# A depthwise convolution tile moved from VectorE to TensorE between the blocks of an mLSTM

## The chip, the cores and the metric

The kernel runs on one core of a Trainium2 chip. The metric is the device time of one execution in microseconds (us). An execution is built from five engines that run their own instruction streams and wait for each other by semaphores: TensorE (PE), VectorE (DVE), ScalarE (ACT), GpSimd (POOL) and SyncE (SP, which here issues most loads).

## The reference

The program is a two-layer backbone on 512 latent and 256 context tokens of width 1024. Only the mixer of layer 0 is touched. It runs a convolution module and a bidirectional mLSTM on the same normed input, and projects both together:

```python
def _dwconv(x, w, b):
    k, ch = w.shape
    pad = (k - 1) // 2
    y = lax.conv_general_dilated(x, w[:, None, :].astype(x.dtype), (1,), [(pad, k - 1 - pad)],
                                 dimension_numbers=('NWC', 'WIO', 'NWC'), feature_group_count=ch)
    return y + b
...
    def merge(p, h_seq):
        a, g, _, _, _, o, _, _ = p
        u = _dwconv(a * jax.nn.sigmoid(g), conv_w, conv_b)
        u = jax.nn.silu(_layer_norm(u, ln_g, ln_b))
        hm = _rms(h_seq).transpose(0, 2, 1, 3)
        hm = hm.reshape(*hm.shape[:2], -1).astype(o.dtype) * head_gain * jax.nn.sigmoid(o)
        return jnp.concatenate([u, hm], axis=-1) @ w_out
```

The convolution is 31 taps wide on 512 channels, so four tiles of 128 channels. `h_seq` is the sum of a forward and a backward mLSTM scan over the tokens, four heads of 128 values each. The layer norm is over all 512 channels: it needs all four tiles.

## The kernel before

All 768 tokens stand along the free dimension, channels along the 128 partitions. A projection (`proj`, `mm`, L110) multiplies in three products, high by high, low by high and high by low, where `weights` (L158 to L168) loads 512 KB of weights (`wr`), rounds them to `wh` on ScalarE and subtracts to `wl` on the engine `lo_eng`, three buffers of each in a ring. `lo_eng` is GpSimd from the start of the mixer to its end. One 128-channel projection of all tokens is 48 matmuls of 384 columns.

`mixer0` (L533 to L737) is written in this order, and the engines keep roughly to it: the projection pair of convolution tile 0 (`glu(0)`: `pa` times the sigmoid of `pg`, whose halves are scaled into `up`), the gates (`pgt`), `glu(1)`, the queries and keys, `glu(2)` and `glu(3)`, then the values (`vproj`, `pv`), among whose four groups of 36 matmuls five units of the modulation vectors are computed (`ada_pe`: 1 MB loads `wa`, matmuls `pada`, a copy `arow` on ScalarE, transposes `pac`, and the bias add into `mods`, on VectorE); one unit is left behind the values. Each `glu` hands its tile to `conv_taps` (L589 to L595): ScalarE writes the first tap into `acc`, VectorE adds the 30 others, one instruction of 783 columns each, called out a few at a time (`TAP`) between the projections. `F` in the order string flushes what is left of them.

Then PSUM is laid out anew (`MLSTM`: two buffers of two banks for `S`, two for `M`), and the string `PAT0` sets the order of three generators: `o`, four output-gate projections (`po`); `m`, the mLSTM, which is five backward state updates (`pu`) and then six steps, each of scores (`pst`), the masked exponentials (`ex`, a DMA, GpSimd and four ScalarE instructions for each of two directions), the readout (`pn`), a forward update, and behind every second step a `finish` (a reciprocal root in small VectorE instructions, eight ScalarE scales of `hu`, transposes `pht` and the gate product into `so`); and `l`, the layer norm (L889 to L938): three adds of tiles, the mean product `pm`, four subtracts, four squares `lsq` with their sum rows `pr`, a root, a broadcast product `pb`, and for each tile a scale, a tanh, an affine step, a product and the split into `uh` and `ul`. Two of the four tiles run on GpSimd. The output projection (`pab`, eight tiles of 48 matmuls) takes the four `uh` as its first half and the mLSTM's `hm` as its second; its first `MH` tiles do their `uh` half ahead of the end of the mLSTM. Everything behind it (the feed-forward part, layer 1) is not touched.

The order string and the way in which a letter becomes work:

```python
PAT0 = 'F' + 'ooommmmmollll' + 'ml' * 22
...
            gens = {"o": [gate_o()], "m": [cell], "l": [ln]}
```

Of the kernel before, what the change touches and what calls it, by code (L numbers as in the profile page):

```python
# [16 lines left out]
P = 128  # L17
# [14 lines left out]
CW = 31  # L32
# [15 lines left out]
MH = 2  # L48
# [3 lines left out]
PAT0 = 'F' + 'ooommmmmollll' + 'ml' * 22  # L52
# [19 lines left out]
MLSTM = {"S": (2, 2), "M": (2, 2)}  # L72
# [8 lines left out]
class Net:  # L81
# [206 lines left out]
    def ada_cols(self, rows, layer, mod, k1):  # L288

        p2 = self.psum1("pac")  # L290
        for k in range(4):
            self.mm(p2[:, 2 * k:2 * k + 2], rows[:, k * P:(k + 1) * P], self.selq, True, True)
        self.ada_bias(p2, layer, mod, k1, 4)

    def ada_first(self, h, pool):

        w = self.d["ada_w"][0]
        for mod in (1, 0):
# [7 lines left out]
            self.ada_cols(self.ada_rows(ps), 0, mod, 4 * h)  # L306
# [61 lines left out]
    def ada_bias(self, p2, layer, mod, k1, n):  # L368
        o = self.mods[layer][:, mod, k1:k1 + n, :]
        k0 = mod * KD + k1  # L370
        b = self.adab[layer][:, k0:k0 + n].unsqueeze(2).to_broadcast([P, n, 2])
        pv = p2[:, :2 * n].rearrange("p (k v) -> p k v", v=2)
        if mod in (1, 4):
            tmp = self.small.tile([P, KD, 2], F32, tag="amod", name=self.name("amod"))[:, :n]
            self.tt(tmp, pv, b, ALU.add)
            self.nc.vector.tensor_scalar(o, tmp, 1.0, None, op0=ALU.add)
        else:
            self.tt(o, pv, b, ALU.add)
# [36 lines left out]
    def setup_c(self, st, sl):  # L415
# [16 lines left out]
        nc.vector.tensor_copy(ab, pa[:, 16:64])  # L432
        self.adab.append(ab)
# [37 lines left out]
    def params(self, st, n):  # L471
# [11 lines left out]
        nc.vector.tensor_scalar(v2[:, 88:89], v2[:, 88:89], float(QK) ** -0.5, None, op0=ALU.mult)  # L483
        self.adab.append(ab)
# [48 lines left out]
    def mixer0(self, pes):  # L533
# [3 lines left out]
        with ExitStack() as es:  # L537
# [60 lines left out]

            def glu(ct):
# [42 lines left out]
            for ct in (2, 3):  # L642
                for _ in glu(ct):
                    self.step(TAP)
                self.step(TAP)
            v1 = self.vproj(win, hs, mods)
# [5 lines left out]
            pes.close()  # L652
            pes = ExitStack()
            self.psum_pool(pes, MLSTM)
# [13 lines left out]
            gens = {"o": [gate_o()], "m": [cell], "l": [ln]}  # L668

            def run(kind):  # L670
                while gens[kind]:
# [3 lines left out]
                    if kind == "c":  # L675
                        return
# [8 lines left out]
            while gens["l"]:  # L685
                run("l")
# [29 lines left out]
            for m in range(KD - KDL):  # L716
                k0 = 4 if m < MH else 0
                w = self.weights(wout, k0, KD - k0, m * P, P)
                ps = pss[m] if m < MH else self.pt("MS"[m // 2 % 2], "pab")[:, 512 - T // 2:512 + T // 2]
# [169 lines left out]
    def layer_norm(self, accs, uh, slot, pslot):  # L889
# [3 lines left out]
        def eng(ct):  # L893
            return nc.gpsimd if ct < 2 else nc.vector
# [45 lines left out]
    def mlstm(self, G, q, k, v1, so, mp):  # L940
# [13 lines left out]
        def update(i, t, old, new):  # L954

            ps = self.pt("M", "pu")
# [629 lines left out]
```

## Time and profile before

| | us |
|---|---|
| median of three runs | 1783.05 |
| lowest, highest | 1782.91, 1785.39 |
| the profiled execution, its own time | 1782.59 |
| span of its profile | 1780.8 |
| PE, DVE, ACT, POOL busy in the span | 1679.1, 1130.3, 679.2, 246.0 |

PE is busy for 94% of the span; the shares of the engines say little of the mixer, which is some 400 us of it. A row of the timeline is start, duration, engine, line, operation, what is written and what is read (names without numbers), its size, how many were joined (x), and in brackets the idle time before it and whose end released it. PE's ends are modelled, so neighbouring matmuls overlap in it: the start-to-start time is the cost.

### The profile page before, as it was taken

What the parts mean: (1) busy time and instruction counts of PE and PEld (TensorE: products, weight loads), DVE (VectorE), ACT (ScalarE), POOL (GpSimd) and SP (SyncE); (2) the same over time, 40 slices, a digit from 0 to 9 for tenths busy, and PEclk for the clock granted to TensorE, in tenths of its full rate; (3) what the DMA queues carried; (4) which work ended last, traced back from release to release, by engine and by line L of the source; (5) the groups of instructions that cost most, each with busy time, mean ns of one, the idle gap of its engine ahead of it and who ended that gap; (6) DMA issues with size and microseconds to landing.
All of it is one profiled execution on the core that took longest, in us unless ns stands there. A gap on an engine that the chain in (4) does not pass through costs nothing.

```text
span 1780.8 us, 24171 instructions
## 1 busy us (share of the span) xinstructions
PE 1679.1 (94%) x9436; PEld 1519.1 (85%) x9436; DVE 1130.3 (63%) x1743; ACT 679.2 (38%) x1364; POOL 246.0 (14%) x331
## 2 busy tenths in 40 slices
PE   6998698769999999999999998999999799999999
PEld 3998476659899999999999878999988788888887
DVE  3799964745876555474334487777788854444544
ACT  4421042542331221212222346777876442332232
POOL 2342132425100000000000111223140200000000
PEclk8999799779999999999999999999999899999999
DMA  9621442233253345262221332001110133333332
GB/s 311 216 61 42 135 143 83 61 118 100 74 159 106 108 142 166 84 200 67 64 60 49 97 96 61 32 13 36 44 35 25 36 95 97 101 98 95 95 95 83
DMA packets 194747, 168.43 MB, mean 95 GB/s; under 512 B 8552, under 2 KB 168214, under 8 KB 194632
## 3 DMA queue, kind: packets, MB, share of 16 engines
q1 hardware_dynamic: 191936, 163.30, 29.8%
q0 software_dynamic: 1280, 3.35, 0.8%
q8 instruction: 75, 1.23, 0.3%
q10 hardware_dynamic: 1416, 0.21, 0.1%
q14 instruction: 40, 0.33, 0.1%
HBM read 161.55 MB, written 5.29 MB: 94 GB/s over the span
## 4 chain that ended last, share of the span: by engine, by line
PE 81%; DVE 10%; DMA 3%; ACT 3%; issue 1%; POOL 1%; SPq 0%; ACTq 0%; DVEq 0%; POOLq 0%
PE pfo L110 17%; PE pfg L110 16%; PE pfv L110 16%; DVE acc L593 6%; PE psc L110 4%; PE pab L110 3%; PE ppv L110 2%; PE pt L1409 2%; PE po L110 2%; PE pf L110 2%; PE pmo L110 2%; PE puq L110 2%; PE pukv L110 2%; PE pv L110 1%; PE pn L110 1%
## 5 line engine op out<-in xcount | busy, mean ns | idle before, releaser
L113 ACT ACTIVATE wh<-wr 128x1024 fp32r<-128x1024 f32 (+3 forms) x205 | 204.4, 999 | 625.0 <-PE pfo L110 215.5
L167 DVE TENSOR_TENSOR wl<-wr,wh 128x1024 fp32r<-128x1024 f32 (+3 forms) x171 | 195.8, 1147 | 194.4 <-ACT wh L113 190.5
L110 PE MATMUL pfo<-hh,wh 128*128 128x384 f32 (+2 forms) x528 | 166.8, 355 | 0.0
L110 PE MATMUL pfo<-hl,wh 128*128 128x384 f32 (+2 forms) x528 | 166.6, 355 | 0.0
L110 PE MATMUL pfo<-hh,wl 128*128 128x384 f32 (+2 forms) x528 | 166.2, 354 | 0.0
L110 PE MATMUL pfg<-fh,wh 128*128 128x384 f32 (+1 forms) x504 | 152.0, 355 | 0.0
L110 PE MATMUL pfg<-fl,wh 128*128 128x384 f32 (+1 forms) x504 | 151.6, 354 | 0.0
L110 PE MATMUL pfg<-fh,wl 128*128 128x384 f32 (+1 forms) x504 | 151.2, 354 | 0.0
L110 PE MATMUL pfv<-fh,wl 128*128 128x384 f32 (+1 forms) x504 | 150.8, 353 | 0.0
L110 PE MATMUL pfv<-fl,wh 128*128 128x384 f32 (+1 forms) x504 | 150.8, 353 | 0.0
L110 PE MATMUL pfv<-fh,wh 128*128 128x384 f32 (+1 forms) x504 | 150.7, 353 | 0.0
L119 DVE SCALAR_TENSOR_TENSOR xr<-pfo,mods,xr 128x512 f32<-128x512 f32 (+1 forms) x128 | 83.7, 665 | 104.4 <-PE pfo L110 103.8
L593 DVE SCALAR_TENSOR_TENSOR acc<-up,par,acc 128x783 f32<-128x783 f32 x120 | 146.9, 1249 | 4.4 <-ACT acc L113 2.3
L167 POOL TENSOR_TENSOR wl<-wr,wh 128x1024 fp32r<-128x1024 f32 (+1 forms) x34 | 85.3, 2512 | 296.9 <-ACT wh L113 280.2
L253 POOL TENSOR_TENSOR ss<-ss,sq 128x256 f32<-128x256 f32 (+1 forms) x31 | 32.1, 1044 | 573.5 <-ACT sq L113 572.6
L119 DVE SCALAR_TENSOR_TENSOR ga<-gr,cc,ga 128x1024 f32<-128x1024 f32 (+1 forms) x84 | 96.0, 1161 | 22.6 <-DMA gr<-in_ada_w_dram 22.3
L110 PEld LDWEIGHTS pfo<-hl,wh 128*128 128x128 f32 x528 | 98.1, 189 | 8.9 <-issue 0.2
L110 PEld LDWEIGHTS pfo<-hh,wh 128*128 128x128 f32 x528 | 97.9, 189 | 9.0 <-ACT hh L113 0.4
L110 PEld LDWEIGHTS pfo<-hh,wl 128*128 128x128 f32 x528 | 97.9, 189 | 8.7
L116 DVE TENSOR_TENSOR ft<-ft,pfv 128x768 f32<-128x768 f32 (+1 forms) x42 | 34.4, 820 | 109.9 <-PE pfv L110 109.9
L110 PEld LDWEIGHTS pfg<-fh,wh 128*128 128x128 f32 x504 | 92.8, 189 | 6.5
L110 PEld LDWEIGHTS pfg<-fl,wh 128*128 128x128 f32 x504 | 92.8, 189 | 6.4
(418 smaller groups left out, 3711.0 us busy)
## 6 DMA issues: line engine op xcount, KB each, us to landing
wr<-in_ffn_w_in_dram SPq DMA_DIRECT2D x88, 512.0 KB, 4.0
gr<-in_ada_w_dram SPq DMA_DIRECT2D x48, 512.0 KB, 4.5
wa<-in_ada_w_dram SPq DMA_DIRECT2D x20, 1024.0 KB, 8.1
wr<-in_ffn_w_out_dram SPq DMA_DIRECT2D x32, 512.0 KB, 3.5
wr<-in_ab_w_in_dram SPq DMA_DIRECT2D x20, 512.0 KB, 5.2
wr<-in_ffn_w_out_dram SPq DMA_DIRECT2D x24, 384.0 KB, 3.3
gr<-in_ada_w_dram SPq DMA_DIRECT2D x16, 256.0 KB, 2.7
wr<-in_mla_w_out_dram SPq DMA_DIRECT2D x8, 512.0 KB, 3.4
```

The source lines that it names most:

```text
L110: self.nc.tensor.matmul(out, lhsT=lhsT, rhs=rhs, start=start, stop=stop)
L113: self.nc.scalar.activation(out, in_, func, **kw)
L116: self.nc.vector.tensor_tensor(out, a, b, op=op)
L119: self.nc.vector.scalar_tensor_tensor(out, a, s, b, op0=op0, op1=op1, **kw)
L167: self.lo_eng.tensor_tensor(lo[:, :n], raw[:, :n], hi[:, :n].bitcast(F32), op=ALU.subtract)
L253: eng.tensor_tensor(self.ss[:, s:e], self.ss[:, s:e], sq[:, s:e], op=ALU.add)
L593: nc.vector.scalar_tensor_tensor(acc[:, :CONVO], up[:, k:k + CONVO], self.convw[:, 4 * k + ct:4 * k + ct + 1], acc[:, :CONVO], op0=ALU.mul ...
L1409: nc.tensor.transpose(pt[:, o:o + P], pe[:, (j + jj) * P:(j + jj + 1) * P], self.ident)
```

## The change

Convolution tile 3 is no longer projected ahead of the values but behind them, as a fourth generator `c`. Its taps are done on TensorE: each tap is a 128 by 128 diagonal matrix (the identity scaled by that tap's column, made by ScalarE), multiplied with the shifted input, in the same three products of high and low parts, 31 taps by 3 products by 512 and 256 columns into one PSUM tile `pcv`, six taps (`DG`) to a letter `c`. ScalarE then adds the convolution's bias on the way out of PSUM. The other parts: the whole mixer keeps one PSUM ring of four two-bank buffers; the low halves of weights go to VectorE from the values on; the layer norm runs wholly on VectorE; the bias of the `ada_pe` units is added by ScalarE, in four instructions of two columns (the `1 +` is folded into the table once); the output projection starts one tile ahead instead of two.

```diff
-MH = 2
+MH = 1
-PAT0 = 'F' + 'ooommmmmollll' + 'ml' * 22
+PAT0 = 'F' + 'cc' + 'mmmmm' + 'mc' * 3 + 'mo' * 4 + 'mc' * 4 + 'mll' * 11
+DG = 6
-MLSTM = {"S": (2, 2), "M": (2, 2)}
...
-        self.ada_bias(p2, layer, mod, k1, 4)
+        self.ada_bias(p2, layer, mod, k1, 4, on_act)
...
+        if on_act:
+            for k in range(n):
+                self.act(o[:, k], pv[:, k], AF.Identity, bias=b[:, k:k + 1])
...
+            def conv_pe(ct, up):
+
+                uph, upl = pslot("uph", F32R), pslot("upl", F32R)
+                self.act(uph[:, :CONVW], up[:, :CONVW])
+                self.tt(upl[:, :CONVW], up[:, :CONVW], uph[:, :CONVW].bitcast(F32), ALU.subtract)
+                taps = self.convw[:, ct:4 * CW:4]
...
+                self.split(taps, th, tl)
+                yield
+                ps = self.psum("pcv")
+                for k0 in range(0, CW, DG):
+                    ks = range(k0, min(k0 + DG, CW))
+                    dh, dl = slot("dh", F32R), slot("dl", F32R)
+                    for i, k in enumerate(ks):
+                        c = slice(i * P, (i + 1) * P)
+                        self.act(dh[:, c], self.ident, AF.Copy, scale=taps[:, k:k + 1])
+                        self.act(dl[:, c], self.ident, AF.Copy, scale=tl[:, k:k + 1])
+                        for j, (w, x) in enumerate(((dh, uph), (dh, upl), (dl, uph))):
+                            for s, e, o in ((0, LAT, 0), (LAT, T, PADC)):
+                                self.mm(ps[:, s:e], w[:, c], x[:, k + s + o:k + e + o], k == 0 and j == 0, k == CW - 1 and j == 2)
+                    yield
+                acc = pslot("acc")
+                nc.gpsimd.memset(acc[:, LAT:LAT + PADC], 0.0)
+                for s, e, o in ((0, LAT, 0), (LAT, T, PADC)):
+                    self.act(acc[:, s + o:e + o], ps[:, s:e], AF.Identity, bias=self.convw[:, 124 + ct:125 + ct])
+                accs.append(acc)
...
+                if ct == 3:
+                    yield from conv_pe(ct, up)
+                    return
...
-            for ct in (2, 3):
-                for _ in glu(ct):
-                    self.step(TAP)
+            for _ in glu(2):
                 self.step(TAP)
...
-            pes.close()
-            pes = ExitStack()
-            self.psum_pool(pes, MLSTM)
+            self.lo_eng = nc.vector
...
-            gens = {"o": [gate_o()], "m": [cell], "l": [ln]}
+            gens = {"c": [glu(3)], "o": [gate_o()], "m": [cell], "l": [ln]}
...
-            return nc.gpsimd if ct < 2 else nc.vector
+            return nc.vector
...
-            ps = self.pt("M", "pu")
+            ps = self.psum("pu")
```

Three places at which the order of instructions moves. The first is ScalarE at the start of the values. `acc` is the first tap of a convolution tile (`up` is its input), `sg` its gate, `arow` a row of a modulation unit, `wh` the high half of weights. Before:

```order
L113 ACTIVATE sg_1278<-pg_1169 128x768
L113 ACTIVATE acc_1288<-up_1280,par 128x783
L113 ACTIVATE wh_1538<-wr_1537 128x1024
L113 ACTIVATE up_1418<-pa_1298 128x512
L113 ACTIVATE up_1418<-pa_1298 128x256
L113 ACTIVATE wh_1609<-wr_1608 128x1024
L113 ACTIVATE sg_1416<-pg_1299 128x768
L113 ACTIVATE arow_1463<-pada_1454 128x512
L113 ACTIVATE acc_1426<-up_1418,par 128x783
```

And with the change, where the tile-2 instruction is `acc_1286`:

```order
L113 ACTIVATE sg_1276<-pg_1167 128x768
L113 ACTIVATE arow_1324<-pada_1315 128x512
L113 ACTIVATE acc_1286<-up_1278,par 128x783
L113 ACTIVATE wh_1547<-wr_1546 128x1024
L113 ACTIVATE mods_111<-pac_1380,adab_194 128x2 x4
L113 ACTIVATE arow_1398<-pada_1389 128x512
L113 ACTIVATE wh_1689<-wr_1688 128x1024
L113 ACTIVATE mods_111<-pac_1454,adab_194 128x2 x4
```

The projection of tile 3 (`up_1418`, `sg_1416`) is gone from here, the first tap of tile 2 stands behind one `arow`, and the bias adds `mods` now stand on ScalarE behind it.

The second is PE where the layer norm's mean product `pm` begins. Before, it stands among the last output-gate projection (`po`) and the backward updates (`pu`), ahead of the first step (`pst`, `pn`):

```order
L110 MATMUL po_2067<-hh_513,wl_2063 128x384 x2
L110 MATMUL pm_2121<-s_240_2117,ones 128x512
L110 MATMUL pu_2050<-v_163_1437,kw_2053 128x258
L110 MATMUL pm_2121<-s_240_2117,ones 128x256
L110 MATMUL pst_2148<-qk_967,qk_1032 128x128 x2
L110 MATMUL pst_2148<-qk_1097,qk_1162 128x128 x2
L110 MATMUL pr_2199<-lsq_2197,sel 6x128 x3
L110 MATMUL pn_2159<-v_162_1436,ex_2125 128x129 x2
```

With the change it stands behind the last convolution products, the first `pht` of a `finish`, and the scores and first readout of the fourth step:

```order
L110 MATMUL pcv_1907<-uph_1806,dl_2613 128x256
L1023 MATMUL pht_2622<-ident,hu_1959 128x128 x4
L1023 MATMUL pht_2622<-ident,hu_2195 128x128 x4
L110 MATMUL pst_2668<-qk_965,qk_1030 128x128
L110 MATMUL pn_2679<-cf,ib_2663 128x129
L110 MATMUL pst_2668<-qk_965,qk_1030 128x128
L110 MATMUL pn_2700<-cf,ib_2663 128x129
L110 MATMUL pst_2668<-qk_1095,qk_1160 128x128 x2
L110 MATMUL pm_2722<-s_305_2675,ones 128x512
```

All four output-gate projections and three steps now precede `pm`.

The third is ScalarE around the layer norm's squares `lsq`. Before, the four stand together behind the mean's copy:

```order
L113 ACTIVATE s_240_2117<-pm_2121 128x768
L113 ACTIVATE lsq_2197<-acc_630 128x768
L113 ACTIVATE lsq_2219<-acc_902 128x768
L113 ACTIVATE lsq_2259<-acc_1288 128x768
L113 ACTIVATE lsq_2308<-acc_1426 128x768
L113 ACTIVATE hu_2158<-pn_2159,dr_2166 128x128
```

With the change the readouts (`hu`) and the exponentials of a later step (`ex_2751`) stand between them:

```order
L113 ACTIVATE s_305_2675<-pm_2722 128x768
L113 ACTIVATE lsq_2739<-acc_628 128x768
L113 ACTIVATE hu_2678<-pn_2679,dr_2688 128x128
L113 ACTIVATE lsq_2780<-acc_900 128x768
L113 ACTIVATE ex_2751<-ex_2751,ccol 128x128
L113 ACTIVATE jk_2694,hss_2443<-hu_2678 128x128
L113 ACTIVATE hu_2678<-pn_2679,dr_2688 128x128
L113 ACTIVATE lsq_2790<-acc_1286 128x768
L113 ACTIVATE ex_2751<-ex_2751,ccol 128x128
```

So the layer norm, which ran beside the output-gate projections and the first three steps, now runs beside the last three.

## Rows read from the trace of the kernel before

**Rows 1.** The page's chain that ended last, by line.
```profile
PE pfo L110 17%; PE pfg L110 16%; PE pfv L110 16%; DVE acc L593 6%; PE psc L110 4%; PE pab L110 3%; PE ppv L110 2%; PE pt L1409 2%; PE po L110 2%; PE pf L110 2%; PE pmo L110 2%; PE puq L110 2%; PE pukv L110 2%; PE pv L110 1%; PE pn L110 1%
```
**Rows 2.** Windows: busy us (count) of PE, PEld, DVE, ACT, POOL; clock, DMA, GB/s.
```profile
173.00:203.00 30.00, 11.43 (x41) 9.00 (x41) 29.50 (x26) 5.09 (x8) 8.36 (x3) 0.67 0.38 123
...
360.00:393.00 33.00, 20.38 (x104) 16.16 (x104) 15.73 (x58) 14.21 (x55) 8.18 (x14) 0.72 0.39 125
```
**Rows 3.** Timeline of PE: end of tile 2's projection, the first two waits among the values.
```profile
146.31 0.51 PE L110 MATMUL pg<-hh,wl 128*128 128x384 f32 x2
...
174.03 0.80 PE L110 MATMUL pv<-wh,hh 128*128 128x512 f32 x1 [5.46 <-ACT up L113]
...
203.11 3.64 PE L110 MATMUL pada<-wa,cc 128*32 128x512 f32 x16 [17.66 <-DVE mods L116]
```
**Rows 4.** Timeline of ScalarE and of VectorE at the same place.
```profile
171.23 1.04 ACT L113 ACTIVATE acc<-up,par 128x783 f32<-128x783 f32 x1 [22.92 <-DVE up L119]
...
170.18 1.02 DVE L119 SCALAR_TENSOR_TENSOR up<-sg,up 128x512 f32<-128x512 f32 x2
```
**Rows 5.** The page's costliest groups: the taps (busy, mean ns).
```profile
L593 DVE SCALAR_TENSOR_TENSOR acc<-up,par,acc 128x783 f32<-128x783 f32 x120 | 146.9, 1249 | 4.4 <-ACT acc L113 2.3
```
**Rows 6.** The chain of waits in order of time: start, us, what.
```profile
214.17 6.62 PE pv L110 x28
...
244.15 1.73 PE pcol L881 x18
246.56 28.79 PE po L110 x150
...
306.44 4.42 DMA ex<-ad
...
353.20 3.35 PE pn L110 x30
...
370.19 0.72 PE pu L110 x2
...
375.76 1.18 PE pst L110 x8
377.30 5.70 PE pn L110 x32
...
393.83 27.47 PE pab L110 x144
...
492.98 8.32 PE pfv L110 x48
```
**Rows 7.** Timeline of PE: matmuls of 512 and 256 columns, back to back.
```profile
450.63 0.39 PE L110 MATMUL pab<-hmh,wl 128*128 128x512 f32 x1
450.86 0.28 PE L110 MATMUL pab<-uh,wh 128*128 128x256 f32 x1
450.98 0.28 PE L110 MATMUL pab<-ul,wh 128*128 128x256 f32 x1
```
**Rows 8.** ScalarE from 252 to 400, groups by operation: ns least/median/most, first and last start.
```profile
L113 ACT ACTIVATE ex<-ex,ccol x40: 384/388/402, 251.9 to 370.7; 128x128 f32<-128x128 f32 x40
...
L113 ACT ACTIVATE lsq<-acc x4: 827/843/845, 293.9 to 298.2; 128x768 f32<-128x768 f32 x4
```
**Rows 9.** Timeline of ScalarE: the scales of the last finish, behind its reciprocal root.
```profile
388.50 2.45 ACT L113 ACTIVATE hu<-hu,hr 128x128 f32<-128x128 f32 x8 [2.24 <-DVE hr L119]
```
**Rows 10.** Timeline of VectorE: operations of the layer norm.
```profile
297.11 1.02 DVE L911 TENSOR_TENSOR acc<-s,acc 128x512 f32<-128x512 f32 x2
...
331.64 0.95 DVE L927 TENSOR_TENSOR acc<-acc,rs 128x768 f32<-128x768 f32 x1
...
347.62 0.68 DVE L931 TENSOR_SCALAR acc<-acc,par 128x768 f32<-128x768 f32 x1
348.33 0.96 DVE L119 SCALAR_TENSOR_TENSOR acc<-th,acc 128x768 f32<-128x768 f32 x1
```
**Rows 11.** The page's DMA issues: KB each, us from issue to landing.
```profile
wa<-in_ada_w_dram SPq DMA_DIRECT2D x20, 1024.0 KB, 8.1
```

More of the change, by code (lines that the diff above doesn't have):

```diff
@@ L286, in ada_rows, with ada_cols @@
         return rows
-    def ada_cols(self, rows, layer, mod, k1):
+    def ada_cols(self, rows, layer, mod, k1, on_act=True):
         p2 = self.psum1("pac")
@@ L305, in ada_first @@
                     self.ada_mm(ps, raw[:, kk], k + kk)
[L306 removed]
+            self.ada_cols(self.ada_rows(ps), 0, mod, 4 * h, False)
     def ada_pe(self, layer, mods, pool):
@@ L366, in ada_sum, with ada_bias, one_plus @@
         self.ada_bias(p2, layer, mod, k1, n)
-    def ada_bias(self, p2, layer, mod, k1, n):
+    def ada_bias(self, p2, layer, mod, k1, n, on_act=False):
         o = self.mods[layer][:, mod, k1:k1 + n, :]
         k0 = mod * KD + k1
-        b = self.adab[layer][:, k0:k0 + n].unsqueeze(2).to_broadcast([P, n, 2])
+        b = self.adab[layer][:, k0:k0 + n]
         pv = p2[:, :2 * n].rearrange("p (k v) -> p k v", v=2)
[L373 to L376, printed above, removed]
-        else:
-            self.tt(o, pv, b, ALU.add)
+        if on_act:
+            for k in range(n):
+                self.act(o[:, k], pv[:, k], AF.Identity, bias=b[:, k:k + 1])
+        else:
+            self.tt(o, pv, b.unsqueeze(2).to_broadcast([P, n, 2]), ALU.add)
+    def one_plus(self, ab):
+        x = ab[:, :48].rearrange("p (m k) -> p m k", k=KD)[:, 1::3]
+        self.nc.vector.tensor_scalar(x, x, 1.0, None, op0=ALU.add)
     def setup(self):
@@ L432, in setup_c @@
         nc.vector.tensor_copy(ab, pa[:, 16:64])
+        self.one_plus(ab)
         self.adab.append(ab)
@@ L483, in params @@
         nc.vector.tensor_scalar(v2[:, 88:89], v2[:, 88:89], float(QK) ** -0.5, None, op0=ALU.mult)
+        self.one_plus(ab)
         self.adab.append(ab)
@@ L597, in mixer0 @@
             accs = []
+            def conv_pe(ct, up):
[3 more added lines that the diff above has]
+                taps = self.convw[:, ct:4 * CW:4]
+                th = self.small.tile([P, CW], F32R, tag="cth", bufs=1, name="cth")
+                tl = self.small.tile([P, CW], F32, tag="ctl", bufs=1, name="ctl")
+                self.split(taps, th, tl)
[17 more added lines that the diff above has]
+                accs.append(acc)
             def glu(ct):
@@ L641, in mixer0 @@
             q, k = self.qkproj(win, hs)
-            for ct in (2, 3):
-                for _ in glu(ct):
-                    self.step(TAP)
+            for _ in glu(2):
                 self.step(TAP)
+            self.step(TAP)
             v1 = self.vproj(win, hs, mods)
@@ L684, in mixer0 @@
                     run(o)
-            while gens["l"]:
-                run("l")
+            for g in "col":
+                while gens[g]:
+                    run(g)
             hes.close()
@@ L983, in finish @@
             yield
-            ps = self.pt("M", "pht")
+            ps = self.psum("pht")
             for j in range(2):
@@ L1029, in mlstm @@
             for pr in range(2):
-                pn = self.pt("M", "pn")
+                pn = self.psum("pn")
                 for i, st in ((0, cf[:, pr] if s else None), (1, cb[:, sb - 1, pr] if sb else None)):
```

6 lines of the change are left out of this document (2 added, 4 removed).

## The prediction

> **What bounds the kernel now.** The first view is the page's chain that ended last: it is PE nearly throughout, and the one large piece that is not is VectorE's taps, 6% of the span [rows 1]. So the question is where the taps hold PE up, and the windows by stage answer it: from 173 to 203 PE is busy for 11.43 us of 30 while VectorE is busy for 29.50 [rows 2]. The timeline of PE names the two waits there, 5.46 us before a value product, released by ScalarE's `up`, and 17.66 us before a `pada`, released by VectorE's `mods` [rows 3]: 23.1 us together. Their cause is VectorE's queue: the second half of tile 2's `up` ran only at 170.18, behind the taps of tiles 0 and 1, and ScalarE's first tap behind it had waited 22.92 us at 171.23, with everything that stands behind it in ScalarE's queue [rows 4]. The 120 taps are 146.9 us of VectorE, ends overlapping [rows 5]; in steps of 1.05 to 1.07 us, some 128.
>
> Behind the values the chain runs through the output gates from 246.56, then alternates between readouts, exponentials' DMAs and updates to 393.83, where the output projection runs without a gap [rows 6]. In the last stretch, 360 to 393, PE is busy for 20.38 us of 33 at a granted clock of 0.72 [rows 2]: the mLSTM's last steps are latency, not work.
>
> **The change, stage by stage.** I keep the clock of the profiled execution and ask when the output projection reaches the point that it has before at 393.83.
>
> *Values.* Tile 3's 30 taps leave VectorE, and its 96 matmuls go behind the values. PE so comes to the values when tile 2's gate products end, at 146.7 [rows 3], 17 us earlier (96 by 0.173, from 48 in 8.32 [rows 6]). But tile 2's `up` still stands behind the same 60 taps, so ends at 171.2, and the first tap on ScalarE still waits for it [rows 4]. The new order puts the four bias adds behind this first tap, on ScalarE, and the next unit's `pada` needs the PSUM buffer that they free. PE's work up to that `pada` is one `pada` of 1.8, 36 value products of 0.236 [rows 3, 6], eight more and a `pac`, some 13 us, so it arrives at 160 and waits until 171.2 + 1.04 (first tap) + 1.04 (`wh`, taken as the first tap) + 1 (bias) = 174.3. A wait of 14.5 us takes the place of 23.1: 8.6 saved. The rest of the taps (tiles 0 to 2 are 90) ends by 211, so no later unit waits for VectorE. On SyncE the last unit's loads now stand behind two weight loads whose buffers wait for VectorE; 8.1 us of landing [rows 11] gives 0 to 3 us of wait; I take none and keep 3 for the range. Values, mods and the moved projection, whose sum was in front before, end at 245.9 (the end of `pcol` [rows 6]) less 8.6 = 237.3.
>
> *Start of the blocks.* Before, the output gates followed at once. Now `pcv` needs tile 3's `sg`, `up` and the four updates that PE has ahead of it: 1.04 + 1.04 + 1.02 [rows 4], and four times two transposes and two products at 0.72 for a product at the low clock [rows 6], about 6 us. The high and low parts of `up` and the first six pairs of diagonals lie beside these. The products begin at about 246.3, where the output gates began before.
>
> *Convolution.* A pair of 512 and 256 columns takes 0.23 + 0.12 [rows 7]; 93 pairs are 32.5 us on PE. The 62 diagonals are 62 by 0.31 = 19 us on ScalarE (0.31 from the eight scales of the same size, 2.45 [rows 9]) and lie beside PE, which needs 6.3 us for six taps against 3.7.
>
> *Up to the last product.* PE has four output gates by 8.32, 33.3; three steps with readout (3.35 to 5.70), scores 1.18 and updates [rows 6], about 6.5 each, 19.5; with the convolution 85.3, and 3 us for waits and slow starts. The last convolution product ends at T = 246.3 + 88.3 = 334.6. These blocks are dense: what were gaps between the output gates and the third step is filled with products, and this is what pays for most of the 32.5 us.
>
> *The tail.* The layer norm cannot begin until T. Before, it ran beside the output gates and the first steps; now it has only the last three steps. From T: ScalarE's bias and three adds (1.02 each [rows 10]) with a gate product between them, 4.2; mean product and copy 2.5, so 6.7; four subtracts at 1.02 with the step's VectorE work, 13.5. The squares of tiles 2 and 3 stand on ScalarE among the readouts and behind the exponentials of a later step, whose DMA takes 4.42 [rows 6] and starts only at T + 12; with four exponentials of 0.39 and two squares of 0.84 [rows 8] the row sums end at T + 24. Root 2.24 alone [rows 9], 5 among the steps' work: T + 29. Broadcast and copy: T + 31. Four tiles of scale, affine step, product and low half, 0.95 + 0.68 + 0.96 + 0.95 = 3.54 each [rows 10], 14.2 and 5.3 of step work: T + 50.5. The last tiles' output products, then the second `finish`: root 2.24, scales 2.45 [rows 9], transposes: T + 60, that is 394.6.
>
> *Output projection.* Of its 384 matmuls before, 48 are done at 393.83; with `MH` at 1 only 24 are. 24 by 0.173 = 4.2 us more behind it.
>
> The other edits: `lo_eng` on VectorE adds about 1.1 us for each load from the values on, beside PE while VectorE idles behind the taps; the one ring of four PSUM buffers I cost at nothing in the forecast, covered while PE is dense; if the cover is gone, it is a rival below.
>
> **Sum.** 394.6 − 393.83 + 4.2 = 5.0 us slower: 1782.59 + 5.0 = 1787.6 for the profiled execution; this one lies 0.46 under the median of 1783.05, so 1788.0.
>
> The weak term is the tail of 60. Its lower bound is what the last three steps took alone, 353.20 to 393.83 [rows 6], 40.6: then T + 40.6, 19.4 less than the forecast, a median of 1768.6. Its upper bound is the same with PE at the low clock, worked out below. I take 60, since every step of it stands in the new order on VectorE or ScalarE, one behind the other.
>
> **Rivals.**
>
> *The layer norm hides.* The subtracts and body go into the gaps of the steps, and the tail is the last three steps (40.6) with the 4.2 ahead of them, 45. Then the output projection is reached 15 us earlier: 5.0 − 15 is 10.0 faster than before, 1773. For it: VectorE is busy for 15.73 us of 33 in the last stretch [rows 2]. Against it: the squares wait for the exponentials, and the body starts only behind the sums of all four.
>
> *The clock falls in the tail.* With the output gates and the convolution used up, PE has only short bursts there. The same readout took 3.35 us in one step and 5.70 in a later one, in a stretch with the clock at 0.72 [rows 2, 6], a mean of 1.2 and 2.4 GHz. Three steps at 5.70 for 3.35 are 7 us on the chain; the other half of a projection tile that was filler is gone as well. I take 6 us over the forecast, 11 slower: 1794. It decides if the mean clock of the tail is under 0.7. The Trainium skill ("TensorE: Matmul & The Clock Gate", section "HAM oscillation — how this bites in real kernels") says that bursts of products with waits between them put the clock back to half, so that each burst starts slowly; it speaks against this change, which takes the filler out of the tail. By that rule the forecast would be this rival's; the row of the last stretch agrees for the kernel before, where the filler is used up in the same way, and so most of it is already in both sides.
>
> *One PSUM ring.* `pcv` keeps one of four buffers from its first to its last product, so score, readout, transposes, update and output gates share three. If each of four buffers a step in three steps waits 1 us for its reader, 12 us over the forecast: 1800. For it: the steps have up to five tiles in flight. Against it: with PE dense, a reader has the 6.3 us of six taps to finish.
>
> *Chances.* The forecast 0.46, the hidden layer norm 0.32, the clock 0.14, the ring 0.08. A difference within 0.2%, 3.6 us, is about what a measurement of this kernel can't tell from none. The forecast's 5.0 stands close above that, so it gives 0.25 slower, 0.18 same, 0.03 faster; the hidden layer norm 0.27 faster, 0.05 same; the clock 0.12 slower, 0.02 same; the ring 0.08 slower. Together 0.30 faster, 0.25 same, 0.45 slower. The range goes from the lower bound of the tail, 1768.5, to the clock's 1794 with the 3 us of loads, 1797; that leaves out most of the ring's case and the ends of the others. The forecast's own range is 1783 to 1793.
>
> **What would show it.** Right: a wait of 12 to 16 us on PE among the values, released by ScalarE, at 160 to 175, and none over 3 us later; `pcv` from 244 to 248, its end at 330 to 338; 62 diagonals with no wait of PE for ScalarE over 1 us; the squares behind the exponentials' DMA; the last `pht` at 390 to 398, and behind it 360 output products without a gap. Wrong: the last `pht` before 383 (the layer norm hides) or after 400; PE waiting for a PSUM buffer in the three dense steps; output products of the first tile waiting for `ul` with the steps done, which would make the layer norm alone the bound; or a wait at the values that stays at 20 us or more, since the bias adds on ScalarE were expected to shorten it only by the work that has moved.

## The result, and the profile after

The changed kernel takes 1801.85 us (median of three runs, 1798.44 to 1802.64) against 1783.05: a ratio of 1.0097, 95% interval 1.0077 to 1.0117. It is slower, as forecast, but by 18.8 us for 5.0, and outside the range. The profiled execution is the lowest of the three, 1798.44, span 1796.7. Its page:

```profile
span 1796.7 us, 24607 instructions
...
PE 1709.0 (95%) x9622; PEld 1545.4 (86%) x9622; DVE 1106.0 (62%) x1730; ACT 704.1 (39%) x1452; POOL 192.2 (11%) x306
...
PE pfo L110 17%; PE pfg L110 16%; PE pfv L110 16%; DVE acc L599 4%; PE pab L110 4%; PE psc L110 3%; PE ppv L110 2%; PE pt L1442 2%; PE pmo L110 2%; PE puq L110 2%; PE pukv L110 2%; PE po L110 2%; PE pf L110 2%; PE pcq L110 1%; PE pv L110 1%; PE pac L110 1%
...
L599 DVE SCALAR_TENSOR_TENSOR acc<-up,par,acc 128x783 f32<-128x783 f32 x90 | 108.9, 1223 | 4.4 <-ACT acc L113 2.2
```

The taps fell from 120 to 90 and from 6% of the chain to 4% [rows 1, 5]: the change does what it says. Its windows (columns as in [rows 2]) and what stands on PE and ScalarE in them:

```profile
146.00:173.00 27.00, 14.21 (x76) 10.43 (x74) 25.12 (x24) 3.46 (x5) 2.84 (x4) 0.82 0.30 98
173.00:203.00 30.00, 28.45 (x142) 18.62 (x143) 29.05 (x27) 6.82 (x19) 2.35 (x1) 0.87 0.53 176
...
236.00:251.00 15.00, 10.61 (x34) 6.00 (x32) 7.88 (x17) 14.09 (x43) 0.11 (x1) 0.70 0.06 19
...
342.70:403.40 60.70, 43.48 (x246) 33.14 (x245) 43.51 (x113) 29.74 (x81) 7.72 (x13) 0.80 0.28 87
```

```profile
171.90 1.04 ACT L113 ACTIVATE acc<-up,par 128x783 f32<-128x783 f32 x1 [22.12 <-DVE up L119]
172.85 1.04 ACT L113 ACTIVATE wh<-wr 128x1024 fp32r<-128x1024 f32 x1
173.79 0.70 ACT L113 ACTIVATE mods<-pac,adab 128x2 f32<-128x2 f32 x4
...
174.55 1.94 PE L110 MATMUL pada<-wa,cc 128*32 128x512 f32 x8 [14.34 <-ACT mods L113]
...
239.39 0.70 PE L110 MATMUL pu<-v,kw 128*128 128x258 f32 x2 [1.39 <-DVE kw L116]
...
250.69 1.20 PE L110 MATMUL pcv<-uph,dh 128*128 128x512 f32 x2
...
342.15 0.52 PE L110 MATMUL pcv<-uph,dl 128*128 128x512 f32 x2
...
384.48 0.98 PE L110 MATMUL pab<-uh,wh 128*128 128x384 f32 x2 [4.73 <-DVE so L119]
...
400.88 1.06 PE L1023 MATMUL pht<-ident,hu 128*128 128x128 f32 x3 [6.55 <-ACT hu L113]
```

The first three rows are the forecast wait, in the forecast order: first tap, weight half, bias. Where the 15.9 us of span went is read from the timelines of PE. The last transposes `pht` end at 391.5 before and 403.4 after, 11.9 later; the output projection behind them ends at 458.0 and 470.2, so takes 0.3 longer; the rest of the program takes 1322.8 and 1326.4, 3.6 longer.

### The profile page after: what moved, and what is told of

It is laid out like the page before. It is cut to its first block, busy times and chain, and to the rows that moved or that the text cites. A ratio compares the mean times of both kernels' runs of the same rounds, so it can differ in the third digit from the quotient of the medians.

```text
span 1796.7 us, 24607 instructions
## 1 busy us (share of the span) xinstructions
PE 1709.0 (95%) x9622; PEld 1545.4 (86%) x9622; DVE 1106.0 (62%) x1730; ACT 704.1 (39%) x1452; POOL 192.2 (11%) x306
## 4 chain that ended last, share of the span: by engine, by line
PE 83%; DVE 10%; DMA 3%; ACT 3%; issue 1%; POOL 0%; SPq 0%; DVEq 0%; POOLq 0%; ACTq 0%
PE pfo L110 17%; PE pfg L110 16%; PE pfv L110 16%; DVE acc L599 4%; PE pab L110 4%; PE psc L110 3%; PE ppv L110 2%; PE pt L1442 2%; PE pmo L110 2%; PE puq L110 2%; PE pukv L110 2%; PE po L110 2%; PE pf L110 2%; PE pcq L110 1%; PE pv L110 1%; PE pac L110 1%
## 5 line engine op out<-in xcount | busy, mean ns | idle before, releaser
L113 ACT ACTIVATE wh<-wr 128x1024 fp32r<-128x1024 f32 (+2 forms) x204 | 204.3, 1004 | 629.8 <-PE pfo L110 223.7
L167 DVE TENSOR_TENSOR wl<-wr,wh 128x1024 fp32r<-128x1024 f32 (+3 forms) x186 | 213.0, 1147 | 235.5 <-ACT wh L113 231.6
L599 DVE SCALAR_TENSOR_TENSOR acc<-up,par,acc 128x783 f32<-128x783 f32 x90 | 108.9, 1223 | 4.4 <-ACT acc L113 2.2
L110 PEld LDWEIGHTS pfg<-fh,wl 128*128 128x128 f32 x504 | 92.8, 189 | 6.5
```

Of the source, the lines that this page charges most:

```text
L110: self.nc.tensor.matmul(out, lhsT=lhsT, rhs=rhs, start=start, stop=stop)
L113: self.nc.scalar.activation(out, in_, func, **kw)
L167: self.lo_eng.tensor_tensor(lo[:, :n], raw[:, :n], hi[:, :n].bitcast(F32), op=ALU.subtract)
L599: nc.vector.scalar_tensor_tensor(acc[:, :CONVO], up[:, k:k + CONVO], self.convw[:, 4 * k + ct:4 * k + ct + 1], acc[:, :CONVO], op0=ALU.mul ...
```

## The experiments

All are read by the same marks on PE's timeline; the table has them for every kernel (us). "Start" is the first convolution product, "last" the end of the last, "ahead" the output products done by the end of the last `pht`, "rest" the span behind the output projection. Each ratio is to the kernel before, on the same chip. The kernel before has medians of 1783.05 to 1785.32 on these chips, so the difference of two experiments' medians can hold some 2 us that belong to the chips. Where the text calls a result the theory's or the rival's, it is that of the expectation above it.

| kernel | median | ratio (95%) | start | last | `pht` | ahead | output | rest |
|---|---|---|---|---|---|---|---|---|
| before | 1783.05 | | | | 391.5 | 48 | 458.0 | 1322.8 |
| changed | 1801.85 | 1.0097 (1.0077, 1.0117) | 250.7 | 342.7 | 403.4 | 25 | 470.2 | 1326.4 |
| e16, changed again | 1804.01 | 1.0106 (1.0085, 1.0127) | 252.1 | 347.7 | 411.0 | 25 | 477.9 | 1326.6 |
| e1 | 1807.44 | 1.0122 (1.0102, 1.0141) | 253.1 | 292.9 | 415.7 | 12 | 483.6 | 1324.4 |
| e2 | 1796.98 | 1.0077 (1.0058, 1.0095) | 252.8 | 334.9 | 400.8 | 25 | 468.1 | 1325.8 |
| e3 | 1781.62 | 0.9984 (0.9973, 0.9995) | 242.8 | 343.2 | 399.0 | 56 | 459.1 | 1323.8 |
| e4 | 1797.95 | 1.0075 (1.006, 1.009) | 249.4 | 342.7 | 400.9 | 25 | 468.1 | 1325.8 |
| e5 | 1801.08 | 1.0087 (1.0068, 1.0106) | 251.8 | 346.0 | 404.0 | 1 | 475.0 | 1324.0 |
| e6 | 1792.71 | 1.0048 (1.0031, 1.0064) | 242.9 | 285.5 | 405.1 | 49 | 467.6 | 1322.9 |
| e7 | 1788.72 | 1.0024 (1.001, 1.0038) | 241.3 | 336.2 | 397.2 | 38 | 460.6 | 1325.0 |
| e8 | 1761.15 | 0.9865 (0.985, 0.988) | 228.8 | 314.8 | 376.0 | 56 | 436.2 | 1322.9 |
| e9 | 1807.84 | 1.013 (1.011, 1.0149) | 257.7 | 353.2 | 413.2 | 25 | 479.9 | 1325.2 |
| e10 | 1781.92 | 0.9982 (0.9972, 0.9991) | | | 396.7 | 56 | 457.3 | 1323.5 |
| e11 | 1780.4 | 0.9979 (0.9965, 0.9994) | 238.8 | 321.6 | 386.4 | 25 | 453.7 | 1325.7 |
| e12 | 1760.43 | 0.9862 (0.9837, 0.9887) | 227.0 | 313.3 | 374.0 | 56 | 434.2 | 1322.9 |
| e13 | 1743.03 | 0.9761 (0.9746, 0.9776) | 228.6 | 290.9 | 353.7 | 56 | 413.9 | 1325.5 |
| e14 | 1768.05 | 0.99 (0.9885, 0.9915) | 230.1 | 316.5 | 374.0 | 48 | 442.1 | 1326.0 |
| e15 | 1771.98 | 0.9921 (0.9901, 0.9941) | 225.8 | 318.0 | 380.5 | 50 | 443.0 | 1329.2 |
| e17 | 1760.3 | 0.9854 (0.9836, 0.9873) | 227.7 | 313.5 | 373.5 | 56 | 433.7 | 1325.7 |
| e18 | 1771.54 | 0.9924 (0.991, 0.9939) | 227.4 | 321.7 | 380.6 | 49 | 443.1 | 1325.7 |

**e1, the convolution ahead of the gates**

```diff
-PAT0 = 'F' + 'cc' + 'mmmmm' + 'mc' * 3 + 'mo' * 4 + 'mc' * 4 + 'mll' * 11
+PAT0 = 'F' + 'cc' + 'mmmmm' + 'mc' * 3 + 'cccc' + 'molll' * 4 + 'ml' * 20
```

> The last three groups of convolution products are put ahead of the output gates instead of behind them, and the layer norm's pieces among the output gates; nothing is added or left out. Theory: the end of the last convolution product (342.7 in the changed kernel) sets the end of the mixer, 60 us of layer norm behind it. Then it ends here near 290, the layer norm lies beside the output gates and steps, the last transposes (403 in the changed kernel) come at 365 to 382, and the whole is 20 to 35 us faster than the changed kernel, about 1765 to 1780. Rival: the last three steps of the mLSTM at a low clock are what takes the 60 us, whatever the layer norm does. Then the dense part ends where it did (342), the last transposes stay at 398 to 404, and the time moves by under 5 us.

Neither came: the convolution ended 50 us earlier, as meant, and the last `pht` 12 us later, 123 us behind it. The end of the convolution alone doesn't set the end.

**e2, one output gate first**

```diff
-PAT0 = 'F' + 'cc' + 'mmmmm' + 'mc' * 3 + 'mo' * 4 + 'mc' * 4 + 'mll' * 11
+PAT0 = 'F' + 'cc' + 'o' + 'mmmmm' + 'mc' * 3 + 'mo' * 3 + 'mc' * 4 + 'mll' * 11
```

> One output gate is put between tile 3's projection and the backward updates, as cover for the chain of updates at the start, which takes 15 us there (236 to 251). Theory: this start is 6 of the 8 us by which the last convolution product was later than forecast, so with a cover the convolution's end and all behind it come 5 to 9 us earlier: 1790 to 1797. Rival: the updates' chain only moves to a later place, because the first step needs it too, and the time stays within 3 us of the changed kernel's.

4.9 us, at the theory's lower edge. The convolution ended 7.8 us earlier, and 5.2 of that were lost again behind it: 65.9 us to the last `pht` for 60.7.

**e3, the two PSUM rings of before**

```diff
+MLSTM = {"S": (2, 2), "M": (2, 2)}
...
+            self.psum_pool(pes, MLSTM)
...
-            ps = self.psum("pst")
+            ps = self.pt("M", "pst")
```

(the same for `pu`, `pn`, `pht`, and the output projection's tiles in pairs by turns, as before.)

> The two PSUM rings of before are brought back, two buffers for updates, scores, readouts and transposes, and two for the rest, of which the convolution's tile keeps one. Theory: the one ring of four costs nothing, since PE shows no wait for a buffer there; two rings can only be the same or slower, by 0 to 12 us, as the output gates then have one buffer while the convolution's is held (each waits 1 us and more for ScalarE's read). Rival: the shared ring is what delays the dense part and the tail; then the time falls by 5 to 12 us.

The rival, by more than it said: 20.2 us between the medians. The two profiled executions lie only 13.8 us apart (1798.44, the lowest of three, and 1784.69, the highest but one of ten), so the traces place a part of it. The window behind the convolution and PE's longest waits in it with two rings, then the waits of the changed kernel (us, times, longest):

```profile
343.20:399.00 55.80, 46.74 (x278) 36.05 (x277) 44.04 (x114) 29.93 (x81) 7.86 (x13) 0.88 0.30 90
```

```profile
PE pm L111 <- DVE s L117: 2.3, 1, 2.3
PE pn L111 <- DVE ex L117: 1.3, 2, 1.1
PE pht L1027 <- DVE hu L120: 0.8, 1, 0.8
```

```profile
PE pht L1023 <- ACT hu L113: 6.6, 1, 6.6
PE pab L110 <- DVE so L119: 4.7, 1, 4.7
PE pm L110 <- DVE s L116: 2.5, 1, 2.5
```

VectorE's work there is the same (44.0 and 43.5 us), and the convolution ends at the same time (343.2 and 342.7). What differs is behind it: 56 output products fill waits instead of 25, and the waits of 6.6 and 4.7 us are gone. In the changed kernel the first output product waits until `so` has read the `pht` before it, which stands on VectorE among the layer norm, and the last step's readout is queued behind that product on PE. (That this wait is itself the loss is not shown; e5 speaks against it.) Of the traces' 11.1 us at the end of the output projection, 31 products by 0.173 [rows 6] are 5.4 and the earlier `pht` is 4.4.

**e4, tile 2's gate product on GpSimd**

```diff
-                    self.stt(u, sg[:, s:e], 1.0, u, ALU.add, ALU.mult)
+                    if ct == 2:
+                        nc.gpsimd.tensor_tensor(sg[:, s:e], sg[:, s:e], u, op=ALU.mult)
+                        nc.gpsimd.tensor_tensor(u, sg[:, s:e], u, op=ALU.add)
```

> Tile 2's gate product is made by GpSimd in four instructions instead of by VectorE in two, so that it no longer stands behind 60 taps; the taps of tiles 0 and 1 stay. Theory: the 14.3 us that PE waits among the values is this queue alone and passes whole to the end; with up done at about 156 the wait falls to 0 to 3 us, and the time falls by 11 to 14 us: 1785 to 1791. Rival: VectorE's taps come due later anyway (the flush of the taps or the later bias adds wait for VectorE), so that the wait only moves behind the values, and under 5 us are gained.

3.9 us, the rival's size, by another wait than it named:

```profile
202.69 1.93 PE L110 MATMUL pada<-wa,cc 128*32 128x512 f32 x8 [9.25 <-DMA wa<-in_ada_w_dram]
```

The last unit's loads `wa` stand on SyncE behind a weight load that waits for VectorE's `wl` and is issued only at 195.98.

**e5, no output projection ahead**

```diff
-MH = 1
+MH = 0
```

> The changed kernel with no output projection ahead of the mLSTM's end (MH 0 for 1). Theory: with one ring, PE loses its time in the tail where the first output product waits 4.7 us for the buffer that VectorE's gate product releases, with the last step's readout queued behind it. Without that product ahead, the last transposes come 4 to 6 us earlier than 403, but 24 products more (4.2 us) stand behind them, so the time is that of the changed kernel within 4 us. Rival: the tail's waits are the layer norm's own chain and the ring's buffers among the steps; then the last transposes stay at 402 to 405 and the time is 3 to 6 us more.

The time is the changed kernel's, as expected, but the last `pht` stayed at 404.0, as the rival had it. The last step's readout in the changed kernel, then in e5:

```profile
386.54 0.71 PE L110 MATMUL pn<-v,ex 128*128 128x129 f32 x2
```

```profile
389.64 0.80 PE L110 MATMUL pn<-v,ex 128*128 128x129 f32 x2 [6.70 <-DVE ex L116]
```

It begins 43.8 us behind the convolution's end there and 43.6 here: a wait for VectorE's `ex` stands where the wait for `so` was. So the queued output product isn't what holds this readout, and from the convolution's end to the last `pht` it took 58.0 us for 60.7.

**e6, two rings and the convolution ahead of the gates** (on e3)

```diff
-PAT0 = 'F' + 'cc' + 'mmmmm' + 'mc' * 3 + 'mo' * 4 + 'mc' * 4 + 'mll' * 11
+PAT0 = 'F' + 'cc' + 'mmmmm' + 'mc' * 3 + 'cccc' + 'molll' * 4 + 'ml' * 20
```

> Two PSUM rings and the convolution's last groups ahead of the output gates. Theory: conv first was slower with one ring only because of the waits for buffers; with two rings the early end of the convolution (293) lets the layer norm run beside the gates, and it is 5 to 12 us faster than two rings alone (1781.6): 1770 to 1777. Rival: the order itself is at fault, since the mLSTM's last steps are then without filler and wait for VectorE and ScalarE; then it is 5 to 25 us slower than two rings alone.

The rival: 11.1 us slower than e3. The last `pht` came 6 us later though the convolution ended 58 us earlier.

**e7, two rings and half of the layer norm on GpSimd** (on e3)

```diff
-            return nc.vector
+            return nc.gpsimd if ct < 2 else nc.vector
```

> Two PSUM rings, and the layer norm's tiles 0 and 1 on GpSimd as before. Theory: VectorE's queue sets the tail, and some 9 us of work of it leave it there: 2 to 5 us faster than two rings alone. Rival: an operation of the layer norm takes GpSimd twice VectorE's time and stands ahead of the masks and products of the steps in its queue, so the time is the same or up to 6 us more.

The rival, and more: 7.1 us slower than e3, 61.1 us behind the convolution's end for 55.8. So with two rings the layer norm is better off on VectorE.

**e8, the gains together** (e2, e3 and e4, and `lo_eng` on GpSimd until the first update)

```diff
-            self.lo_eng = nc.vector
...
+                if i == PAT0.index('m'):
+                    self.lo_eng = nc.vector
```

> Two PSUM rings, one output gate ahead of the backward updates, tile 2's gate product on GpSimd, and the low halves of weights left on GpSimd until the first update, so that the last modulation unit's loads do not stand behind weight loads that wait for VectorE (a 9.3 us wait of PE for a load took the place of the one removed where tile 2's product was on GpSimd alone). Theory: the gains add, 5 for the gate and 9 to 13 for the values: 1764 to 1770. Rival: GpSimd's queue (four subtracts of 2.5 us among the values) replaces VectorE's, or the gain ends at the tail, and it stays at 1773 to 1782.

The theory, and 3 us more: 23.8 us faster than before on its chip (1784.91), so it beats both kernels. No wait is left on PE among the values over 0.8 us, and the start is dense. Windows of the start and of the stretch behind the convolution:

```profile
220.00:235.00 15.00, 14.79 (x85) 13.49 (x83) 5.16 (x7) 14.57 (x41) 0.11 (x1) 1.00 0.18 52
314.80:376.00 61.20, 50.12 (x282) 39.71 (x282) 47.19 (x120) 32.80 (x91) 10.75 (x16) 0.83 0.31 94
```

**e9, the bias of the units back on VectorE**

```diff
-        self.ada_bias(p2, layer, mod, k1, 4, on_act)
+        self.ada_bias(p2, layer, mod, k1, 4)
```

> The changed kernel with the bias adds of the modulation units back on VectorE, where the first stands behind six more taps and the next behind ten. Theory: PE's first wait among the values grows from 14.3 us by 5 to 7, later ones by 0 to 3, and all of it passes to the end: 5 to 9 us slower than the changed kernel, 1806 to 1811. Rival: the wait only takes time from the wait for the last unit's loads and the start of the blocks, so under 3 us more.

```profile
183.27 3.60 PE L110 MATMUL pada<-wa,cc 128*32 128x512 f32 x16 [23.40 <-DVE mods L116]
```

The theory. The wait is 9.1 us longer, about the two of before together [rows 3], and the output projection ends 9.7 later; the median is 6.0 higher. Most of the wait passes on.

**e10, the kernel before with one ring**

```diff
-            self.psum_pool(pes, MLSTM)
...
-            ps = self.pt("M", "pst")
+            ps = self.psum("pst")
```

(the same for `pu`, `pn` and `pht`, and the output projection's tiles by `psum_even`.)

> The kernel before with one thing of the change: the one PSUM ring of four buffers instead of two rings of two. No convolution product is in it, so no tile is held for long. Theory: what costs 20 us in the changed kernel is that the long-held tile leaves three buffers, and that output products ahead of the end need a buffer that a late VectorE instruction frees; here the ring has four, and it costs 0 to 4 us: 1783 to 1789. Rival: the ring by itself, which mixes the short tiles of the mLSTM with those that wait long for a reader, costs as much here: 8 to 20 us slower than before.

The theory: the ring alone costs nothing here; these runs lie 2.6 us under before (1784.57 on the same chip). The last `pht` comes 5.2 us later, but 56 output products for 48 are done ahead, and the output projection behind it takes 60.6 us for 66.5.

**e11, e8 with one ring**

```diff
-            self.psum_pool(pes, MLSTM)
...
-            ps = self.pt("M", "pst")
+            ps = self.psum("pst")
```

(and the others as in e10.)

> The combined kernel (1761.15) with the one PSUM ring of the change again. Theory: the ring's price stands in the tail behind the convolution, which this kernel has too, so it costs 10 to 20 us again: 1771 to 1781. Rival: it cost that only with the changed kernel's late start, and here under 5.

19.3 us, the theory. In the trace (span 20.3 longer): the first convolution product, which in PE's order again stands behind four updates, as many as the ring has buffers, comes 10.0 us later, and the last one 6.7; behind it 3.7 more to the last `pht`, 7.1 more in the output projection (25 products ahead for 56), 2.8 in the rest.

**e12, the layer norm's low halves on GpSimd, in e8**

```diff
-            eng(ct).tensor_tensor(lo, a, hi.bitcast(F32), op=ALU.subtract)
+            (nc.gpsimd if ct < 3 else nc.vector).tensor_tensor(lo, a, hi.bitcast(F32), op=ALU.subtract)
```

> The combined kernel (1761.15) with the layer norm's low halves of tiles 0 to 2 on GpSimd, nothing else of it. Theory: VectorE's queue sets the tail (47 us busy of 61), so 2.9 us less of it, with a longer instruction only at the end of each tile, gives 1 to 4 us: 1757 to 1760. Rival: the output products wait for the longer GpSimd instruction, or the tail is the steps' own chain, and the time is the same or up to 3 us more.

The rival: 0.7 us, less than such runs tell apart.

**e13, one of three products, in e8**

```diff
-                        for j, (w, x) in enumerate(((dh, uph), (dh, upl), (dl, uph))):
+                        for j, (w, x) in ((2, (dh, uph)),) if k else ((0, (dh, uph)),):
```

> The combined kernel (1761.15) with one of the three products of each tap, the high parts alone; 62 of 93 pairs, 21.7 us of PE, are left out, the diagonals stay. Theory: PE is dense from the values to the last convolution product, and that product's end sets the rest, so its end (314.8) comes 18 to 22 us earlier and so does the whole: 1739 to 1744. Rival: the products lie in gaps between the mLSTM's steps, and under 8 us are gained: 1753 to 1761.

The theory: 18.1 us of the 21.7 left out. The convolution's products are on the path nearly in full.

**e14, e8 with the output projection in the projections' ring alone**

```diff
-                ps = pss[m] if m < MH else self.pt("MS"[m // 2 % 2], "pab")[:, 512 - T // 2:512 + T // 2]
+                ps = pss[m] if m < MH else self.psum_even("pab")
```

> The combined kernel (1761.15) with its two rings, but the output projection's tiles all in the ring of the projections, as none of the mLSTM's buffers. Theory: of the 19 us that one ring costs there, the 31 output products that then don't fit ahead of the end are 5; here as many are done ahead of the last transposes as in the changed kernel (25 for 56) and it is 3 to 7 us slower: 1764 to 1768. Rival: the products are put ahead just the same, or the tail takes no notice: within 2 us.

6.9 us slower, the theory's size, but 48 products were still ahead, and the `pht` came earlier than in e8. The loss is behind it: 68.0 us to the end of the output projection for 60.2. The 8 products fewer are 1.4 of it, and PE waits once, as in the kernel before:

```profile
376.37 1.65 PE L111 MATMUL pab<-hmh,wh 128*128 128x384 f32 x4 [2.34 <-ACT hmh L114]
```

So the output tiles' share of buffers counts; the count ahead alone is not its measure.

**e15, the last tile left out of the mean and variance, in e8**

```diff
-        for a in accs[2:]:
+        for a in accs[2:3]:
...
-        for ct in range(4):
+        for ct in range(3):
```

(with the `l` letters among the gates, and tile 3's subtract ahead of its scale.)

> The combined kernel (1761.15) with the layer norm's mean and variance over tiles 0 to 2 alone, so that its statistics can be done beside the gates and before the last convolution product; the last tile's share of the statistics is left out, the work on the four tiles stays. Theory: the layer norm's chain from the last product is what makes the tail 61 us; then the tail falls to 38 to 50 and the whole to 1738 to 1750. Rival: the last three steps of the mLSTM, with VectorE's work on them, take those 60 us by themselves, as with the convolution first; then the tail stays at 55 to 62 and the time at 1755 to 1762.

The rival as to the tail: 62.5 us behind the convolution's end for 61.2, although the mean product now stands 23 us ahead of that end. The time, 10.8 us slower, is above both ranges; of the traces' 13.1 us, 6.3 lie in the rest of the program. VectorE had less to do in the tail:

```profile
318.00:380.50 62.50, 44.75 (x222) 35.57 (x222) 40.90 (x109) 26.13 (x76) 9.47 (x15) 0.75 0.26 80
```

**e16, the changed kernel once more**

> The changed kernel itself once more. Theory: 3 to 4 us of its loss behind the mixer (drift of the granted clock in the feed-forward part, in the profiled execution) is chance of that execution, so that the new profile differs there by some us either way, while its mixer is the same within 1.5 us (output projection's end at 470); the median lies at 1798 to 1802. Rival: the drift belongs to the kernel and comes again, 3 us at the same places.

The rival for the rest, which came again to 0.2 us; and against both, the mixer differs by 7.6 us between two executions of one kernel. Whether the rest belongs to the kernel isn't settled, as e8 and e17, which differ in a buffer count, show 1322.9 and 1325.7.

**e17 and e18, four buffers for the exponentials, in e8 and in e15**

```diff
-            ex = [mp.tile([P, 4, P], F32, tag="ex", bufs=3, name=self.name("ex")) for _ in range(2)]
+            ex = [mp.tile([P, 4, P], F32, tag="ex", bufs=4, name=self.name("ex")) for _ in range(2)]
...
-                    jk = mp.tile([P, P], F32, tag="jk", bufs=1, name=self.name("jk"))
+                    jk = ex[0][:, 2 * pr + b]
```

> The combined kernel (1761.15) with four buffers for the mLSTM's exponentials instead of three (the squares' unused output goes into a used one of them), so that the next step's two loads need not wait for the readout before. Theory: the 60 us behind the convolution's end are three steps of the mLSTM, whose chain of load, mask, exponentials, scores, readout and update takes some 19 us each when nothing fills it, with VectorE at 47 of 61 us close behind; the loads then leave the chain and 2 to 6 us are gained: 1755 to 1759. Rival: VectorE's work alone is what bounds it here, or the loads were early already: within 2 us.

> The kernel in which the last tile is left out of the layer norm's statistics (1771.98), with four buffers for the exponentials. Theory: there the tail (62.5 us) has VectorE busy for 41 alone, and its chain holds one load of the exponentials (3.9 us) with the mask and the exponentials behind it; four buffers take 5 to 12 us out: 1760 to 1767. Rival: the order on PE, fixed beforehand, is what holds it, and the time stays within 3 us.

The rival both times: 0.9 and 0.4 us, less than such runs tell apart. The loads' buffers are not it.

## Why the prediction was wrong

**The values** came as worked out: a wait of 14.34 us (forecast 14.5) released by ScalarE's `mods` at 174.55 (174.3), tile 3's projection done at 236.1 (237.3). e9 shows that the gain is the bias adds' move to ScalarE: 23.40 without it. No wait for the last unit's loads showed, within its 0 to 3.

**The start** was mis-sized: 9.0 us forecast from the projection's end to the first product, 14.6 measured. The updates ahead of `pcv` took 11.3 us (239.39 to 250.69) and not 6, in a stretch at a clock of 0.70, a mean of 1.2 and 2.4 GHz. Of those 6 us, eight products at 0.72 are 5.8, so next to nothing was left for the transposes, the first step's scores and the waits for `kw` and `cb`, four of them here, 2.2 us together. ScalarE, busy for 14.09 of those 15 us, isn't what held the first product, since its inputs were there long before: the first diagonals by 239, `uph` by 240.0 and `upl` by 241.1. e3 and e11 point to what I had not seen: with two rings the first products stand among the updates and start 8 and 10 us earlier, with one ring behind them. In e3 that gained nothing at the convolution's end (343.2 for 342.7), against e8 in e11 it cost 6.7.

**The dense part** took 92.0 us from the first product to the last, 88.3 forecast. e13 agrees with its working: products left out come off the path.

**The tail** was 60.7 us for 60, with a wrong reason. I took every step of the layer norm as one behind the other from the convolution's end, and its lower bound from the last three steps of before. e15 takes the last tile out of the statistics and the tail stays; in e1 and e6 the convolution ends 50 and 58 us earlier and the end does not follow. So the layer norm's chain is not its only bound, and that the number came out was luck. The hidden-layer-norm rival fell with it. What does hold these 55.8 to 66 us, with three steps in them and VectorE busy for 41 to 47, is open: not the loads' buffers (e17, e18), not VectorE's low halves (e12).

**The clock** did not fall: 0.80 in the changed kernel's tail. The same length ahead of the last `pht` of the kernel before:

```profile
331.00:391.50 60.50, 43.54 (x240) 35.95 (x240) 38.06 (x111) 31.30 (x101) 19.15 (x22) 0.81 0.36 105
```

The Trainium skill's rule ("TensorE: Matmul & The Clock Gate", section "HAM oscillation — how this bites in real kernels"), that bursts between waits start slowly, agrees with both rows alike, so it prices no difference here.

With two rings the tail's clock is 0.88 (e3) and 0.83 (e8), so a part of what the ring costs may be clock; no run takes the two apart.

**The output projection** was to cost 4.2 us for 24 products more; from the last `pht` on, 0.3 showed (66.5 us for 336 products before, 66.8 for 359). The kernel before has a wait there that the change hasn't:

```profile
393.83 1.65 PE L110 MATMUL pab<-hmh,wh 128*128 128x384 f32 x4 [2.35 <-ACT hmh L113]
```

The sum set the end of the new transposes against 393.83, behind this wait. From that mark on, 64.2 us became 66.8, 2.6 more.

**The sum** of the profiled execution was 5.0 and 15.9 came. By its own marks the difference is the start, 5.6 more than forecast, the dense part 3.7, the tail 0.7 and the rest of the program 3.6, less 1.2 of the values and 1.6 of the output projection. The ring, at nothing in the forecast, has no mark of its own: what it costs stands inside these terms, and only e3 and e11 tell it apart.

**The failed step** is "the one ring of four PSUM buffers I cost at nothing in the forecast". Taken away it gives back 20.2 us (e3), put into e8 it costs 19.3 (e11). Without it the rest of the change is not slower at all (0.9984, interval 0.9973 to 0.9995), so that the change came out slower, as forecast, was luck.

The rival of the ring had the size, 1800, at a chance of 0.08. Its reason was not shown: it put the waits into the dense steps, where `pcv` holds a buffer, but with two rings the last product of the changed kernel comes at the same time. What both pairs show alike is the output projection, 66.8 us with one ring for 60.1 with two (e3) and 67.3 for 60.2 (e11), with 25 products ahead for 56; and e14, which only takes the output tiles out of the mLSTM's ring, costs 6.9. What is left is open: e3's traces have 4.9 in the tail and 2.7 in the rest, e11's 6.7 at the convolution's end, 3.7 in the tail and 2.8 in the rest. Leaving out e1 and e6, whose convolution is early, the tails overlap: 58.0 to 65.9 us with one ring, 55.8 to 62.8 with two. e10 shows that the ring by itself costs nothing in the kernel before. That it costs where the layer norm, the last steps and the output tiles want buffers at the same time fits these runs, but is not shown.

## What to carry over

A ring of PSUM buffers has to be priced by who stands behind whom when it runs full. Here two rings, one for the mLSTM's short tiles with every other pair of output tiles, one for the rest, were 19 to 20 us better than one (e3, e11). Ask it anew for each change, since the same ring was free in the kernel before (e10). And a tail that has the forecast length does not confirm the chain that was summed to it: leave a link of the chain out and see if it shortens.

## What was not expected of the hardware

Two executions of the changed kernel end the output projection at 470.2 and 477.9, with the same instructions in the same order on PE, VectorE, ScalarE and GpSimd; and the four runs of e16, on one chip, lie between 1800.9 and 1808.51. And the rest of the program, where PE has the same instructions in the same order, moved by 3.6 us. About 1.5 of them come in a stretch of the feed-forward part where PE is busy throughout: around the products `pac` of a modulation vector (128x2 each) the granted clock is lower, 0.89 before (first row) and 0.80 in the changed kernel. Why it differs is open.

```profile
640.00:655.00 15.00, 15.00 (x89) 15.00 (x89) 8.53 (x11) 3.10 (x4) 0.00 (x0) 0.89 0.56 176
```

```profile
653.00:670.00 17.00, 17.00 (x93) 17.00 (x92) 8.74 (x9) 3.55 (x4) 0.00 (x0) 0.80 0.50 155
```
